# The last two sums of a 64x64 inverse: from identity products on TensorE and copies on ScalarE to additions on VectorE

## The chip, the core and the metric

The kernel runs on one core of one Trainium2 chip. The metric is the device time in microseconds (us) of one execution. A time is the median of the runs shown; the profile is of one execution more, with its own time and span. A core has five engines with a queue each, worked off in order: TensorE (PE in the rows; PEld is its loading of stationary operands), VectorE (DVE), ScalarE (ACT), GpSimd (POOL) and SyncE (SP), which issues the loads and stores.

## What is computed

Two trunk layers over 1024 latent and 256 context tokens. In each layer one input projection feeds a retention head group and an RWKV-7 head group; their gated outputs go through one output projection. The change lies in the RWKV-7 scan, which the reference writes as one step per token:

```
def step(s, inp):
    r_t, w_t, k_t, v_t, kap_t, a_t = inp
    s_kap = jnp.einsum('bhvk,bhk->bhv', s, kap_t)
    s = (s * w_t[:, :, None, :]
         - s_kap[..., None] * (kap_t * a_t)[:, :, None, :]
         + v_t[..., None] * k_t[:, :, None, :])
    return s, jnp.einsum('bhvk,bhk->bhv', s, r_t)
...
    s_fin, y = lax.scan(step, s0, xs, reverse=reverse)
```

## The kernel before

The scan is done in chunks of 64 tokens. Within a chunk the dependence of each token on the earlier ones is a triangular 64x64 system, whose inverse is worked out ahead of the scan. A head pair has 10 steps (of two chunks, two directions and two heads: eight inverses side by side, four matrices of 128 partitions by 64 columns); there are four head pairs and two layers, so 80 steps in all.

Three functions make a step. `prep` loads features and scales them. `prep2` multiplies them (`pm`, then `gq`), and inverts. `seq` is the recurrence proper: it multiplies with the state, takes `z2`, the finished inverse, and updates `uv` and the state `st`. `prep2` runs three steps ahead of `seq`, on two lanes in turn: a lane has one PSUM bank `pinv`, whose halves are `q` and `tp`. Between the steps the program deals out the projections (`pproj`, lines 493 to 495) and the other work of the layer as filling.

The inverse goes like this. The matrix (I plus `gq`) is split into two f16 parts `hi` and `lo`. Six levels build an approximate inverse in f16: line 1001 multiplies `hi` into `tz`, VectorE masks the bank to `xx` (line 1015), line 1017 multiplies with `ttb`, ScalarE copies to `tz` (line 1018), VectorE transposes to `tt` (lines 1021 and 1028). Then the remainder is formed: line 1030 makes the product of `hi` and `lo` with `tz`, less the identity, in the bank, and ScalarE writes its negative to `eb` (line 1033). Two corrections follow: `z1 = tt + e^T tt` and `z2 = tt + e^T z1`. Each of these two sums is done by the helper `one_sum`: a 128x256 product of the identity `one16` with `tt` opens the bank (line 990), four 128x64 products with `eb` add to it (line 993), and ScalarE copies the bank to `z1` (f16) or `z2` (f32). Rows of the profile name both of these tiles `z`, since they leave trailing numbers out; line 1037 is `z1` and line 1040 is `z2`.

The order of instructions on each engine is laid out when the program is built, by a scheduler that picks among ready work by a timeline of its own; `prep2` and `seq` are given priority over the filling.

Of the kernel before, what the change touches and what calls it, by code (L numbers as in the profile page):

```python
# [12 lines left out]
F16 = mybir.dt.float16  # L13
AF = mybir.ActivationFunctionType
ALU = mybir.AluOpType
# [110 lines left out]
def hybrid_kernel(ctx: ExitStack, tc: tile.TileContext, a: dict, out: bass.AP, dbg: dict | None = None):  # L126
    nc = tc.nc
# [3 lines left out]
    const = ctx.enter_context(tc.tile_pool(name="const", bufs=1))  # L131
# [7 lines left out]
    def bank(tag, name):  # L139
        return ps.tile([128, 512], F32, tag=tag, name=name, bufs=BANKS[tag])  # L140
# [6 lines left out]
    def behind(ins, first):  # L147
        tc.add_manual_dep(ins.ins, first.ins.name, mybir.DependencyInfo(mybir.DependencyClass.NoSync, mybir.DependencyReason.DATA),
                          reason="the first product of a bank clears its written bits")
# [15 lines left out]
    def x_tile(tb):  # L165
        t = ln_pool.tile([128, D], F32, tag="xt", name="xt", bufs=XTB)
        load(t, a["ctx"][0, 128 * tb:128 * tb + 128, :] if tb < 2 else a["x"][0, 128 * (tb - 2):128 * (tb - 2) + 128, :])
        return t
# [4 lines left out]
    def cload(name, shape):  # L173
        t = const.tile(shape, F32, name=name)
        load(t, a[name])
        return t

    ident = cload("c_id", [128, 128])
# [7 lines left out]
    kdix = cload("c_kd", [128, 4])  # L186
    keep = cload("c_rs", [128, 256])
    id16 = const.tile([128, 64], F16, name="id16")
    one16 = const.tile([128, 128], F16, name="one16")
    neg16 = const.tile([128, 128], F16, name="neg16")  # L190
    nc.vector.tensor_copy(one16, ident)
    nc.vector.tensor_scalar(neg16, ident, -1.0, None, ALU.mult)
    lvm = const.tile([128, 2, 6, 64], F16, name="lvm")
    nc.vector.tensor_copy(id16[0:64], ident[0:64, 0:64])
# [32 lines left out]
    def turn(key):  # L227
        at[key] += 1
        return ring[key][(at[key] - 1) % len(ring[key])]
# [144 lines left out]
    for l in range(DEPTH):  # L374
# [55 lines left out]
        if l == 0:  # L430
            lp = ln_pool
            stage = [lp.tile([128, 8, 128 * len(tiles)], F32, name=f"xs{ci}") for ci, tiles in enumerate(LN_TILES)]
            for ci, tiles in enumerate(LN_TILES):
# [5 lines left out]
                for i, tb in enumerate(tiles):  # L439
                    t = x_tiles[tb] if tb < XTB else x_tile(tb)  # L440
# [7 lines left out]
                for k in range(8):  # L448
                    p = bank(("inv", "m")[k % 2], "pxt")
# [500 lines left out]
        def prep2(sp, c):  # L950
# [7 lines left out]
            for h in range(2):  # L958
                pm[h] = quad(bank("m", f"pm{h}"))
                for i in range(2):  # L960
                    for d in range(2):
                        nc.tensor.matmul(pm[h][:, i, d, 0:q1], bk[HR[h], i, d, :], own[HR[h], i, d, 0:q1],  # L962
                                         start=True, stop=True)
# [16 lines left out]
            q, tp = [pc[:, 256 * k:256 * k + 256].rearrange("p (i d t) -> p i d t", i=2, d=2) for k in range(2)]  # L980
            ID = [(i, d) for i in range(2) for d in range(2)]
# [6 lines left out]
            def one_sum(lhs, rhs, parts):  # L988

                one = nc.tensor.matmul(pc[:, 0:256], lhs, rhs, start=True, stop=False, skip_group_check=True)  # L990
                for n, (w, x) in enumerate(parts):
                    for i, d in ID:
                        behind(nc.tensor.matmul(q[:, i, d, :], w[:, i, d, :], x[:, i, d, :], start=False,
                                                stop=n == len(parts) - 1, skip_group_check=True), one)
# [3 lines left out]
            for n in range(6):  # L998
# [14 lines left out]
                else:  # L1013
# [5 lines left out]
                    if n < 5:  # L1019
                        tt = sp.tile([128, 2, 2, 64], F16, tag=f"tt{lane}", name="tt", bufs=1)  # L1020
# [10 lines left out]
            e = turn("eb")  # L1031
            for h in range(2):
                nc.scalar.activation(idr(e[HR[h], :, :, 64 * h:64 * h + 64]), idr(q[HR[h]]), AF.Copy, scale=-1.0)
            flat = lambda t: t.rearrange("p i d t -> p (i d t)")
            one_sum(one16, flat(tt), [(e, tt)])
            z1 = sp.tile([128, 2, 2, 64], F16, tag="z1", name="z1", bufs=1)
            nc.scalar.copy(z1, q)
            one_sum(one16, flat(tt), [(e, z1)])
            z2 = sp.tile([128, 2, 2, 64], F32, tag="z2", name="z2", bufs=ZB)
            nc.scalar.copy(z2, q)  # L1040
            c.update(gq=gq, bt=bt, z2=z2)

        def seq(sp, cur, nxt, st, ys):
# [200 lines left out]
        def ahead(g):  # L1244
            p, s = divmod(g, NT)
            if p < NP:
                need(p, ready)
                stages[g] = prep(sp, p, s)
            if 0 <= g - 1 < NP * NT:
                with tc.high_priority(offset=1000):  # L1250
                    prep2(sp, stages[g - 1])
# [64 lines left out]
```

## Time and profile before

| | |
|---|---|
| median of 3 runs | 2461.8 us (2458.17 to 2465.19) |
| profiled execution | 2462.74 us, of which the span from first to last instruction is 2460.7 us |
| TensorE busy | 2299.2 us, 93% of the span |
| VectorE, ScalarE, GpSimd busy | 1735.6, 1414.8 and 1319.7 us (71%, 57%, 54%) |
| mean granted TensorE clock | 0.964 |

A busy time is the union of an engine's instructions. A matmul's row lasts from its start to the end of its results, so consecutive matmuls overlap in the rows; what a matmul holds back is the distance from its start to the next start. A wait is idle time of an engine and is put down to what ended last before it.

### The profile page before, as it was taken

The numbers are of one execution on the slowest core, as the hardware profiler recorded it, in microseconds if no ns is written. First come the engines' busy times: TensorE is split into PE (matmuls) and PEld (weight loads), VectorE is DVE, ScalarE is ACT, GpSimd is POOL, SyncE is SP. The second block draws the span as 40 slices with busy tenths as digits, with TensorE's granted clock in tenths as the row PEclk, the third lists the DMA queues.
The fourth block names the chain that finished last, engine by engine and source line by source line (L and its number), as shares of the span: only waits on it lengthen the run. The fifth ranks groups of instructions, "written<-read, shape, count | busy, mean of one in ns | idle before, by whom it ended". The sixth has DMA issues, their size and how long they took to land.

```text
span 2460.7 us, 69593 instructions
## 1 busy us (share of the span) xinstructions
PE 2299.2 (93%) x25463; PEld 1739.9 (71%) x25463; DVE 1735.6 (71%) x4784; ACT 1414.8 (57%) x4261; POOL 1319.7 (54%) x2032
## 2 busy tenths in 40 slices
PE   5779999999999999999997899999999999998997
PEld 2357776877788777778655687778768877776855
DVE  2646686787678867777648677767867886669756
ACT  3455664565566655456546666646655665456663
POOL 1455564465556654456536556545654665456662
PEclk7888999999999999999998899999999999999998
DMA  8754443334334423335533543434433443334544
GB/s 313 270 187 110 117 118 87 113 108 124 78 89 139 126 70 92 75 100 154 176 108 123 152 130 112 108 94 119 128 87 100 124 124 80 79 88 120 143 130 128
DMA packets 539606, 302.77 MB, mean 123 GB/s; under 512 B 238995, under 2 KB 526465, under 8 KB 537217
## 3 DMA queue, kind: packets, MB, share of 16 engines
q1 hardware_dynamic: 539264, 298.33, 42.1%
q8 instruction: 201, 3.29, 0.6%
q14 instruction: 141, 1.15, 0.2%
HBM read 212.21 MB, written 85.98 MB: 121 GB/s over the span
## 4 chain that ended last, share of the span: by engine, by line
PE 58%; DVE 13%; DMA 6%; ACT 4%; issue 3%; POOL 2%; SPq 2%; DVEq 0%; POOLq 0%; ACTq 0%
PE pproj L493 8%; PE pproj L495 8%; PE pproj L494 8%; PE pseq L1061 8%; PE pm L962 5%; DMA ft<-feat 2%; PE pseq L1053 2%; PE pinv L1001 2%; PE pinv L1017 2%; PE pout L821 1%; PE pout L823 1%; PE pss L638 1%; PE pout L822 1%; PE pss L648 1%; PE pyt L1127 1%
## 5 line engine op out<-in xcount | busy, mean ns | idle before, releaser
L493 PE MATMUL pproj<-h_hi,whi 128*128 128x256 f16 (+2 forms) x2128 | 631.3, 298 | 9.1 <-ACT craw L505 5.1
L494 PE MATMUL pproj<-h_lo,whi 128*128 128x256 f16 (+2 forms) x2128 | 629.1, 297 | 7.6 <-DVE h_lo L365 7.1
L495 PE MATMUL pproj<-h_hi,wlo 128*128 128x256 f16 (+2 forms) x2128 | 627.2, 297 | 0.7 <-POOL wlo L320 0.7
L320 POOL TENSOR_TENSOR wlo<-wraw,whi 128x256 f16<-128x256 f32 x360 | 250.5, 707 | 208.7 <-ACT wraw L319 181.0
L495 PEld LDWEIGHTS <-wlo 128*128 128x128 f16 x2128 | 213.5, 100 | 76.5 <-issue 12.1
L494 PEld LDWEIGHTS <-whi 128*128 128x128 f16 x2128 | 212.6, 100 | 77.6 <-issue 18.6
L493 PEld LDWEIGHTS <-whi 128*128 128x128 f16 x2128 | 213.1, 100 | 75.3 <-issue 10.4
L986 POOL COPY ttb<-tt 64x256 f16<-64x256 f16 x320 | 139.1, 436 | 205.2 <-DVE tt L1021 160.5
L1015 DVE TENSOR_TENSOR xx<-pinv,lvm 128x256 f16<-128x256 f32 x400 | 164.3, 416 | 90.6 <-PE pinv L1001 87.4
L318 ACT ACTIVATE whi<-wraw 128x256 f16<-128x256 f32 x360 | 139.2, 412 | 132.9 <-PE pproj L494 61.1
L1018 ACT CAST tz<-pinv 128x256 f16<-128x256 f32 x400 | 146.1, 370 | 119.9 <-PE pinv L1017 107.7
L962 PE MATMUL pm<-own,bk 64*128 64x128 f32 (+1 forms) x1280 | 201.6, 294 | 8.3 <-DVE bk L942 4.0
L1021 DVE STREAM_TRANSPOSE tt<-tz 128x256 f16<-128x256 f16 x320 | 139.4, 437 | 97.0 <-ACT tz L1018 94.3
L976 POOL TENSOR_TENSOR il<-gq,c_id 64x256 f32<-64x256 f32 x160 | 120.1, 751 | 133.1 <-DVE gq L965 119.3
L986 ACT COPY ttb<-tt 64x256 f16<-64x256 f16 x320 | 128.6, 402 | 106.5 <-DVE tt L1021 102.1
L962 PEld LDWEIGHTS pm<-own,bk 64*128 64x128 f32 x1280 | 163.2, 193 | 33.1 <-issue 8.6
L965 DVE TENSOR_TENSOR gq<-pm,c_m 128x256 f32<-128x256 f32 (+1 forms) x320 | 115.7, 402 | 50.6 <-PE pm L962 49.8
L1061 PE MATMUL pseq<-st,own 64*64 64x64 f32 x2432 | 149.4, 228 | 0.0
L319 ACT ACTIVATE wraw<-wraw 128x256 f32<-128x256 f32 x376 | 146.3, 410 | 3.9
L1001 PEld LDWEIGHTS <-hi 128*128 128x128 f16 x1920 | 104.6, 99 | 41.6 <-issue 9.7
L1012 POOL TENSOR_TENSOR lo<-il,hi 64x256 f16<-64x256 f32 x160 | 113.5, 710 | 36.8 <-ACT hi L977 28.0
L1008 POOL TENSOR_TENSOR ttb<-hi,lvm 128x256 f16<-128x256 f16 x160 | 113.6, 729 | 19.0 <-ACT hi L977 18.2
(255 smaller groups left out, 5906.7 us busy)
## 6 DMA issues: line engine op xcount, KB each, us to landing
ft<-feat SPq DMA_DIRECT2D x320, 160.0 KB
wraw<-in_w_in_dram SPq DMA_DIRECT2D x264, 128.0 KB
feat<-zth SPq DMA_DIRECT2D x80, 256.0 KB
wm<-in_w_mod_dram SPq DMA_DIRECT2D x16, 1024.0 KB
wraw<-in_w_out_dram SPq DMA_DIRECT2D x112, 128.0 KB
lap<-la SPq DMA_DIRECT2D x40, 256.0 KB
uv<-vt SPq DMA_DIRECT2D x320, 32.0 KB
wm<-in_w_mod_dram SPq DMA_DIRECT2D x16, 512.0 KB
```

What stands on the lines that cost most here:

```text
L319: nc.scalar.activation(raw, raw, AF.Copy, scale=WS)
L320: nc.gpsimd.tensor_tensor(lo, raw, hi, ALU.subtract)
L493: nc.tensor.matmul(p[:, 0:n], hi[:, k, :], h_hi[:, kk, m0:m1], start=first, stop=False)
L494: nc.tensor.matmul(p[:, 0:n], hi[:, k, :], h_lo[:, kk, m0:m1], start=False, stop=False)
L495: nc.tensor.matmul(p[:, 0:n], lo[:, k, :], h_hi[:, kk, m0:m1], start=False, stop=stop)
L962: nc.tensor.matmul(pm[h][:, i, d, 0:q1], bk[HR[h], i, d, :], own[HR[h], i, d, 0:q1], start=True, stop=True)
L986: eng(idr(dst[HR[h], :, :, 64 * h:64 * h + 64]), idr(src[HR[h]]))
L1001: nc.tensor.matmul(q[:, i, d, :], hi[:, i, d, :], id16 if n == 0 else tz[:, i, d, :], start=True, stop=True)
L1015: nc.vector.tensor_tensor(xx, q, mk, ALU.mult)
L1018: nc.scalar.copy(tzn, tp)
L1021: nc.vector.transpose(idr(tt), idr(tzn))
L1061: rm = nc.tensor.matmul(pq[HR[h], k, d, :], lhs, rhs, start=False, stop=stop, skip_group_check=True)
```

## The change

The identity product is left out of both sums. The four products with `eb` now open the bank themselves, and VectorE adds bank and `tt` into `z1` and `z2`, where ScalarE had copied the bank. `one16` and the copy that fills it go; the first sum, with `neg16`, stays as it is.

```
-    one16 = const.tile([128, 128], F16, name="one16")
     neg16 = const.tile([128, 128], F16, name="neg16")
-    nc.vector.tensor_copy(one16, ident)
...
-            flat = lambda t: t.rearrange("p i d t -> p (i d t)")
-            one_sum(one16, flat(tt), [(e, tt)])
+            for i, d in ID:
+                nc.tensor.matmul(q[:, i, d, :], e[:, i, d, :], tt[:, i, d, :], start=True, stop=True)
             z1 = sp.tile([128, 2, 2, 64], F16, tag="z1", name="z1", bufs=1)
-            nc.scalar.copy(z1, q)
-            one_sum(one16, flat(tt), [(e, z1)])
+            nc.vector.tensor_tensor(z1, q, tt, ALU.add)
+            for i, d in ID:
+                nc.tensor.matmul(q[:, i, d, :], e[:, i, d, :], z1[:, i, d, :], start=True, stop=True)
             z2 = sp.tile([128, 2, 2, 64], F32, tag="z2", name="z2", bufs=ZB)
-            nc.scalar.copy(z2, q)
+            nc.vector.tensor_tensor(z2, q, tt, ALU.add)
             c.update(gq=gq, bt=bt, z2=z2)
```

The scheduler lays out every queue anew, so places shift all over the program. Line numbers after the change are two lower up to the inverse's end, and one lower behind it.

On TensorE, at the first correction of the tenth inverse of the first layer, the queue before the change reads so (`whi` is a weight of the projections, `eb` the remainder):

```order
L494 LDWEIGHTS whi
L494 MATMUL pproj<-h_lo,whi 128x256
L990 LDWEIGHTS one_97
L990 MATMUL pinv<-tt,one_97 128x256
L993 LDWEIGHTS eb_1780
L993 MATMUL pinv<-tt,eb_1780 128x64
```

And at the same correction after it (`pyt` belongs to the readout of an earlier step):

```order
L493 LDWEIGHTS wlo
L493 MATMUL pproj<-h_hi,wlo 128x256
L1126 MATMUL pyt<-c_id,yc 64x64 x3
L1033 LDWEIGHTS eb_1778
L1033 MATMUL pinv<-tt,eb_1778 128x64
```

The weight load of `one` and its product are gone, and the four products with `eb` stand directly behind other work.

On VectorE, at the end of the same inverse, before the change, no instruction of the two sums stands in the queue (`uv` and `st` are the recurrence, `kkd` and `gs` the retention and gate work, `yc` and `yb` the readout):

```order
L1081 COPY uv<-pseq 64x2x64
L688 SCALAR_TENSOR_TENSOR gs<-gth,pproj 128x256
L1093 SCALAR_TENSOR_TENSOR st<-pseq,f,sf 128x64 x2
L1098 TENSOR_TENSOR ym<-pseq,ym 128x64 x2
L1113 TENSOR_TENSOR yc<-ym,gsm 128x128
L618 SCALAR_TENSOR_TENSOR sbp_1799<-sbp_1798,cd,sbp_1799 128x64
L1113 TENSOR_TENSOR yc<-ym,gsm 128x128
L1138 TENSOR_TENSOR yb<-yb,bo 128x256
```

After the change the two additions (`z_5787` is `z1`, `z_5793` is `z2`) stand among these:

```order
L1080 COPY uv<-pseq 64x2x64
L1112 TENSOR_TENSOR yc<-ym,gsm 128x128 x2
L1035 TENSOR_TENSOR z_5787<-pinv,tt 128x256
L686 SCALAR_TENSOR_TENSOR gs<-gth,pproj 128x256
L1137 TENSOR_TENSOR yb<-yb,bo 128x256
L1092 SCALAR_TENSOR_TENSOR st<-pseq,f,sf 128x64 x2
L1097 TENSOR_TENSOR ym<-pseq,ym 128x64 x2
L616 SCALAR_TENSOR_TENSOR sbp_1797<-sbp_1796,cd,sbp_1797 128x64
L1138 SCALAR_TENSOR_TENSOR yb<-yb,gt 128x256
L1039 TENSOR_TENSOR z_5793<-pinv,tt 128x256
L963 TENSOR_TENSOR gq<-pm_6154,c_m_88 128x256 x2
```

`z1` now stands ahead of the state's update `st`, and `z2` ahead of the masking `gq` of a later step.

## Rows read from the trace of the kernel before

**Rows 1.** The page: busy by engine, then 40 slices, then the chain.

```profile
PE 2299.2 (93%) x25463; PEld 1739.9 (71%) x25463; DVE 1735.6 (71%) x4784; ACT 1414.8 (57%) x4261; POOL 1319.7 (54%) x2032
...
PE   5779999999999999999997899999999999998997
...
PE 58%; DVE 13%; DMA 6%; ACT 4%; issue 3%; POOL 2%; SPq 2%; DVEq 0%; POOLq 0%; ACTq 0%
```

**Rows 2.** Busy time by stretch: the two layers' scan stretches, all engines.

```profile
182.00:1247.00 1065.00, 1033.86 (x12078) 808.19 (x12078) 779.92 (x2215) 624.00 (x1902) 592.38 (x920) 0.98 0.39 110
1387.00:2412.00 1025.00, 984.91 (x11321) 753.31 (x11323) 755.52 (x2111) 617.49 (x1887) 588.45 (x918) 0.98 0.40 111
```

**Rows 3.** Timeline of PE, 417.2 to 418.2 us: start, duration, engine, line.

```profile
417.25 0.27 PE L494 MATMUL pproj<-h_lo,whi 128*128 128x256 f16 x1
417.36 0.28 PE L1017 MATMUL pinv<-xx,ttb 128*128 128x64 f16 x4
417.48 0.27 PE L495 MATMUL pproj<-h_hi,wlo 128*128 128x256 f16 x1
417.59 0.27 PE L493 MATMUL pproj<-h_hi,whi 128*128 128x256 f16 x1
417.70 0.27 PE L990 MATMUL pinv<-tt,one 128*128 128x256 f16 x1
417.81 0.28 PE L993 MATMUL pinv<-z,eb 128*128 128x64 f16 x4
418.02 0.39 PE L1053 MATMUL pseq<-uv,gq 128*64 128x64 f32 x6
```

**Rows 4.** Line 990, the identity products: count, nanoseconds min/median/max.

```profile
L990 PEld LDWEIGHTS <-one x160: 94/98/180, 218.3 to 2411.2; 128*128 128x128 f16 x160
L990 PE MATMUL pinv<-tt,one x160: 269/273/437, 218.5 to 2411.5; 128*128 128x256 f16 x160
```

**Rows 5.** Tile pinv: the readers of the bank, nanoseconds min/median/max.

```profile
L1015 DVE TENSOR_TENSOR xx<-pinv,lvm x400: 377/417/427, 184.2 to 2398.5; 128x256 f16<-128x256 f32 x134
...
L1037 ACT CAST z<-pinv x80: 347/372/406, 219.3 to 2410.5; 128x256 f16<-128x256 f32 x80
L1040 ACT COPY z<-pinv x80: 348/372/418, 227.4 to 2411.9; 128x256 f32<-128x256 f32 x80
```

**Rows 6.** Waits of PE, 182 to 2412 us: total us, times, longest.

```profile
PE pinv L1017 <- DVE xx L1015: 7.9, 13, 1.4
PE pseq L1061 <- DVE uv L1081: 7.0, 8, 2.5
...
PE pinv L1001 <- ACT tz L1018: 5.6, 9, 1.0
...
PE pinv L990 <- ACT z L1037: 0.9, 3, 0.5
```

**Rows 7.** Tile pseq: the recurrence's copy to uv on DVE.

```profile
L1081 DVE COPY uv<-pseq x160: 292/293/294, 232.2 to 2425.1; 64x128 f32<-64x128 f32 x160
```

**Rows 8.** Waits of ACT, whole span: total us, times, longest.

```profile
ACT z L1040 <- PE pinv L993: 30.7, 31, 3.0
...
ACT z L1037 <- PE pinv L993: 17.3, 21, 2.9
```

**Rows 9.** Busy time by stretch: where VectorE is fullest, as in rows 2.

```profile
680.00:820.00 140.00, 140.00 (x1756) 116.38 (x1752) 115.80 (x342) 87.20 (x255) 81.71 (x119) 1.00 0.40 112
1840.00:2000.00 160.00, 154.86 (x1927) 129.50 (x1927) 130.83 (x380) 102.33 (x313) 94.85 (x144) 1.00 0.40 111
```

**Rows 10.** Busy time by stretch around one spell of low granted clock.

```profile
1030.00:1037.00 7.00, 5.51 (x93) 4.56 (x93) 6.83 (x26) 3.67 (x12) 3.79 (x7) 0.99 0.56 133
1037.00:1058.00 21.00, 20.70 (x160) 15.76 (x161) 11.40 (x31) 8.73 (x32) 7.50 (x13) 0.52 0.16 45
```

## The prediction

> **What bounds the kernel now.** I read the page first: TensorE is busy 93% of the span, its slices are full from the fourth to the end but for the turn between the layers, and the chain that ended last runs through it for 58% [rows 1]. The reader should not stop at that figure, because a matmul's row overlaps the next. So the second view is busy time by stretch. In the two scan stretches, 2090 us together, TensorE shows nothing running in 71.2 us (1065 - 1033.9 and 1025 - 984.9); VectorE is busy 1535 us there, 73.5%, ScalarE 1241 us, 59%; both have room on average [rows 2]. In a full stretch, 680 to 820 us, TensorE has no gap at all [rows 9]. The third view is the timeline, for what a product really holds back: 128x256 products start 0.11 us after each other though each row lasts 0.27, and they do so without pause [rows 3]. Where a queue starts its work back to back, what is taken out of it comes off the time. The fourth view is TensorE's list of waits: its largest entries on the recurrence and the inverse are 7.9, 7.0 and 5.6 us in all [rows 6]. So in the stretches that the change touches TensorE's own work is the bound, with a few short waits on VectorE and ScalarE between.
>
> **The change part by part.** *The identity products.* 160 of them go, two in each of 80 steps [rows 4]. One holds back the next start by 0.11 us: 417.70 to 417.81 [rows 3]. The same rows show that nothing reappears in its place: line 1017 is also a set of four 128x64 products right behind a projection, and it starts 0.11 us after it and lets the next start 0.12 us later; its loads are covered by the product ahead. The load of `one` was covered as well, so its 0.098 us [rows 4] is worth nothing. Sum: 160 x 0.11 = 17.6 us less on TensorE. If the row's full 0.273 us counted it would be 43.7; I don't take that, since the next product starts long before.
>
> *The copies on ScalarE.* 160 x 0.372 = 59.5 us less [rows 5]. ScalarE is not the bound, and TensorE waited for the copy to `z1` three times, 0.9 us [rows 6]. What stands behind these copies gets earlier, `tz` above all, for which TensorE waits 9 times in 400 [rows 6]. At that frequency it is 160 x 9/400 x 0.37 = 1.3 us; I take zero, and 1.3 as the bound.
>
> *The additions on VectorE.* There are 160, each reading 128x256 f32 from the bank and 128x256 f16 from a tile. The trace has this form already: line 1015, 377 to 427 ns, median 417 [rows 5]. `z2` writes f32 in place of f16; the two copies on ScalarE, f16 and f32 out, both take 372 [rows 5], so I price it the same. That is 160 x 0.417 = 66.7 us more work, 0.83 us a step. Per link of the chain it is 0.045 us slower than the copy; twice a step, 7.2 us over all, if the inverse were the path; it runs three steps ahead of its use, so I count that at nothing.
>
> What of the 66.7 us comes to the path? First, TensorE can wait for the new result itself. For line 1015 that cost 7.9 us in 400, 0.02 each [rows 6]; 160 x 0.02 = 3.2 us. Second, what is queued behind: in the new order `z1` stands ahead of `st` and `z2` ahead of `gq`, with `uv` in the neighbourhood. TensorE was held by `uv` 8 times [rows 6] in 160 [rows 7], 5%. If an addition of 0.42 us stands before such a moment in each case, 160 x 0.05 x 0.42 = 3.4 us. Bounds: nothing, if the additions fall into VectorE's idle quarter; all 66.7, if each holds TensorE for its whole length. The first is much nearer to what line 1015 shows, so I take 6.6 us.
>
> *The fill of `one16`* is one small copy in the start-up, where VectorE is not full; nothing. The first sum with `neg16` is untouched.
>
> The sum: 2462.7 (the profiled execution) - 17.6 + 6.6 = 2451.7. The profiled execution lies 0.9 over the median of the runs, so I expect a median of **2451 us**, 0.4% less.
>
> [...]
>
> **The rivals.** *The work saved falls into gaps (no change).* If the step is paced by the recurrence through `w`, `uv` and `st`, or by the two lanes of the inverse, TensorE's queue only waits 0.11 us longer at the next product of the chain. For it: 71.2 us of gaps in the scan [rows 2], four times what is saved, and short waits below the length of a row that the busy time doesn't show. Against it: 680 to 820 us without a gap [rows 9]. If three quarters of the 17.6 us are lost so and the 6.6 us are paid, the time is 2462.7 - 4.4 + 6.6 - 0.9 = 2464; if nothing is paid, 2457.
>
> *VectorE's queue holds up the recurrence (slower).* The place is the additions in front of `uv` and `st`. ScalarE stood idle 30.7 and 17.3 us ahead of the two copies, waiting for the products [rows 8]; now VectorE's queue stands there, and everything behind it, in stretches where it is already busy 115.8 of 140 us [rows 9]; five to six steps there add 4.7 us, 86%. It cancels the gain when an addition keeps TensorE for 17.6/160 = 0.11 us on average, 26% of its length, and makes the kernel slower by 0.3% from (17.6 + 7.4)/160 = 0.156 us, 37%. At half of its length the time is 2461.8 - 17.6 + 33.4 = 2478. Against it: line 1015, in the same queue, costs 0.02 us each.
>
> *A larger gain.* The granted clock falls to half in spells: 0.52 from 1037 to 1058 us, behind 7 us in which TensorE was busy 5.5, and in these 21 us some 10 are lost [rows 10]. The new order can lose or add such a spell. With the whole 17.6 us, ScalarE's 1.3 and one spell less: 2461.8 - 28.9 = 2433. A spell more puts the forecast at 2461, among the no-change cases.
>
> **How the numbers follow.** What a measurement can tell from no change is 0.3%, 7.4 us: 2454.4 and 2469.2 are the limits. The forecast, 2442 to 2454, gets 0.56; the larger gain 0.07; work lost in gaps or a spell more 0.24; VectorE's queue 0.13. So faster 0.63, same 0.24, slower 0.13. The range from 2437 to 2469 leaves out most of the slower case and the far end of the larger gain, some 2 in 10.
>
> **What the profile after would show.** Right: 160 matmuls fewer; in the scan TensorE's starts 0.11 us apart with projection and `eb` products adjoining; VectorE's two lines at 0.42 us, busy total near 1802 us; ScalarE near 1355; TensorE's waits for VectorE up by less than 10 us. Wrong: waits of TensorE for `uv`, `st`, `xx` or the products with `z` grown by 20 us or more (the slower rival), or its gaps in the scan grown by as much as its work fell, with no single waiter (the no-change rival). The forecast fails if an addition takes far over 0.42 us, or if spells of low clock differ by more than one between the two traces.

## The result: 0.4 to 0.7% slower, and the profile after

The changed kernel takes 2477.5 us (median of 6 runs, 2470.6 to 2487.5) against 2459.7 us for the kernel before (6 runs): ratio 1.0074, 95% interval 1.0048 to 1.0101. A later comparison of the same queues (g0 below), 12 runs against 29 on one chip, gave 1.0042 [1.0018, 1.0065]. The prediction was 2451 us and faster; both the sign and the range (up to 2469) failed.

The page of the changed kernel: the line of busy times and the line of the granted clock in 40 slices.

```profile
PE 2309.5 (93%) x25303; PEld 1739.8 (70%) x25303; DVE 1746.0 (70%) x4943; ACT 1370.0 (55%) x4101; POOL 1321.3 (53%) x2032
...
PEclk7888999999999999999998899999999999988997
```

The reader is to see the work moved as the change says: 160 matmuls fewer than in [rows 1], ScalarE 45 us less. Yet TensorE's busy time is 10 us more, not less. Busy time grows when the clock falls, since each product lasts longer (a row of 258 columns takes 0.27 us at a granted clock of 1.00 and 0.42 us at 0.50, in the timeline below). The view of the cores shows the mean granted clock of the changed kernel:

```profile
core 0: 2477.6 us, clock 0.953
```

Before, 2460.7 us ran at 0.964. If all that ran in a low stretch went at half speed, the clock took the span times (1 - clock): 2477.6 x 0.047 = 116.4 us after, 2460.7 x 0.036 = 88.6 us before, 28 us more. The span grew by 17 only, so by this measure the rest of the kernel got 11 us shorter, which is the sum of the prediction (17.6 - 6.6 = 11.0). That agreement is luck in part: the measure charges 2.5 us for each 0.001 of clock, and the runs of one kernel show 1.7 (ahead of the table below). By that price the clock took some 18 us and the rest got some 2 us shorter. Busy time by stretch, for the same stretches as [rows 2] and the second of [rows 9] (PE, PEld, DVE, ACT, POOL, then the granted clock):

```profile
182.00:1247.00 1065.00, 1031.50 (x12016) 800.84 (x12015) 788.10 (x2297) 599.38 (x1824) 591.97 (x919) 0.99 0.40 109
1387.00:2412.00 1025.00, 985.17 (x11140) 751.05 (x11138) 750.56 (x2166) 595.62 (x1802) 589.83 (x916) 0.96 0.40 110
...
1840.00:2000.00 160.00, 159.99 (x1873) 131.27 (x1870) 126.45 (x379) 96.64 (x294) 90.50 (x135) 0.94 0.40 111
```

The first layer's scan is as it was, a little better in clock. Most of the loss is in the second layer's, where the clock fell from 0.98 to 0.96, and TensorE got through 11140 products where before it got through 11321, 181 fewer; only some 80 of these had been taken out there. From 1840 to 2000 us before had 1.00.

Tile pinv of the changed kernel, the two new additions (ns min/median/max), and the waits of TensorE from 182 to 2412 us (total, times, longest), which answer to [rows 5] and [rows 6]:

```profile
L1035 DVE TENSOR_TENSOR z<-pinv,tt x80: 385/418/427, 220.9 to 2416.3; 128x256 f16<-128x256 f32 x80
L1039 DVE TENSOR_TENSOR z<-pinv,tt x80: 384/416/427, 226.3 to 2417.2; 128x256 f32<-128x256 f32 x80
```

```profile
PE pseq L1060 <- DVE uv L1080: 6.6, 7, 2.7
...
PE pinv L1015 <- DVE xx L1013: 4.4, 9, 0.9
...
PE pinv L1037 <- DVE z L1035: 1.7, 3, 1.0
...
PE pinv L999 <- DVE z L1039: 1.3, 4, 0.6
```

The additions take the 0.417 us of the prediction, TensorE waits 3.0 us for them in all (3.2 were predicted), and the waits for `uv` and `xx` did not grow. TensorE shows nothing running for 73.3 us in the two scan stretches, 71.2 before. No wait explains the 17 us.

What one fall of the clock looks like: busy time by stretch, 1887 to 1905 us of the changed kernel, and the timeline of PE around the fall (start, duration, line).

```profile
1887.00:1890.00 3.00, 3.00 (x50) 2.51 (x47) 2.29 (x7) 2.28 (x6) 0.00 (x0) 1.00 0.14 45
1890.00:1892.50 2.50, 2.50 (x32) 2.18 (x29) 2.16 (x7) 0.73 (x3) 1.09 (x2) 1.00 0.55 160
1892.50:1895.00 2.50, 2.50 (x19) 1.76 (x18) 1.35 (x4) 0.77 (x2) 1.18 (x2) 0.76 0.17 58
1895.00:1902.50 7.50, 7.50 (x50) 6.22 (x50) 3.28 (x12) 1.81 (x5) 4.62 (x9) 0.50 0.12 35
```

```profile
1889.78 0.45 PE L1060 MATMUL pseq<-w,z 64*64 64x64 f32 x8
1890.16 1.10 PE L960 MATMUL pm<-own,bk 64*128 64x64 f32 x8
1891.19 0.45 PE L1060 MATMUL pseq<-st,own 64*64 64x64 f32 x8
1891.57 0.71 PE L636 MATMUL pss<-qt,kt 64*128 64x128 f32 x4
1892.12 0.38 PE L639 MATMUL pss<-sbp,qt 64*128 64x128 f32 x2
1892.43 0.23 PE L999 MATMUL pinv<-tz,hi 128*128 128x64 f16 x2
...
1893.54 0.27 PE L493 MATMUL pproj<-h_hi,wlo 128*128 128x258 f16 x1
...
1893.94 0.42 PE L493 MATMUL pproj<-h_hi,wlo 128*128 128x258 f16 x1
```

TensorE shows no gap in these 15.5 us (a row runs to the end of its results, so a pause shorter than a row would not show), and still the granted clock drops to half, 0.50 from 1895 to 1902.5 us. From 1889.78 to 1893.54 us stand narrow products only, 128 columns or fewer and nearly all f32, of the recurrence and the attention; the first wide one behind them still takes 0.27 us, and from 1893.94 us on they take 0.42.

This fall is not the usual one. The trace has sixteen falls between 182 and 2412 us, and in the 4 us ahead of fourteen of them TensorE stood idle for 0.4 to 3.5 us, as at 2187 us behind a wait of 1.38 us for VectorE. In the kernel before it stood idle for 0.8 to 3.3 us in the 4 us ahead of all ten ([rows 10] is one of them). So 2 of the 26 falls in these two traces have no such gap ahead, this one and the one at 1928 us.

### The profile page after: what moved, and what is told of

It is laid out like the page before. It is cut to its first block, busy times and chain, and to the rows that moved or that the text cites. A ratio compares the mean times of both kernels' runs of the same rounds, so it can differ in the third digit from the quotient of the medians.

```text
span 2477.6 us, 69184 instructions
## 1 busy us (share of the span) xinstructions
PE 2309.5 (93%) x25303; PEld 1739.8 (70%) x25303; DVE 1746.0 (70%) x4943; ACT 1370.0 (55%) x4101; POOL 1321.3 (53%) x2032
## 5 line engine op out<-in xcount | busy, mean ns | idle before, releaser
L999 PE MATMUL pinv<-tz,hi 128*128 128x64 f16 x1600 | 112.7, 195 | 10.0 <-DVE tz L1002 6.0
```

The costliest lines, as they stand in the source:

```text
L999: nc.tensor.matmul(q[:, i, d, :], hi[:, i, d, :], id16 if n == 0 else tz[:, i, d, :], start=True, stop=True)
```

## The experiments

Two things could explain this: the scheduler laid every queue out anew (the prediction gave that no price), or the change itself costs, by VectorE or by the clock. To part them, most kernels below hold all instructions that two kernels share to the places that they have in one kernel's queues. The program is built once for its order, and then again with an edge between neighbours of each engine's queue:

```diff
+    _, queues = program(*DONOR, None)
+    nc, got = program(*TARGET, queues)
...
+                for q in queues.values():
+                    for x, y in zip(q, q[1:]):
+                        tc.add_manual_dep(told[y], told[x].name, _mybir.DependencyInfo(_mybir.DependencyClass.NoSync, _mybir.DependencyReason.DATA),
```

Only the identity products, the copies and the additions differ then. "Old order" has the queues of the kernel before, "new order" those of the changed kernel.

The results together. "Clock" is the mean over a kernel's runs. "At full clock" is the mean over runs of time times clock; it counts every low stretch as if all in it went at half speed, 2.5 us for each 0.001 of clock. That is too much: over the 254 runs, taken within each kernel, the time falls by 1.68 +- 0.07 us for each 0.001 ("+-" is one standard error throughout). So differences stand below at both prices, "at full clock" and "at equal clock", which is the difference of the mean times less 1.68 us for each 0.001 by which the clocks differ. As most falls stand behind a wait (24 of the 26 above), which costs time of its own, it is not shown that even the smaller price is the clock's alone.

The kernel before stood in each of the four comparisons at 2459 to 2461 us, clock 0.963 to 0.9645, at full clock 2370 to 2371. Each comparison had a chip of its own: f1, f2, f3 and g1; g0, g2 and g3; d1, k1 and DUE 31; e1, e3 and RAMP 6.

| kernel | order | identity products, sum by | median us | ratio to before [95%] | clock | at full clock |
|---|---|---|---|---|---|---|
| g0, the change | new | none, VectorE | 2473.3 | 1.0042 [1.0018, 1.0065] | 0.9553 | 2362.6 |
| g1 | new | one, ScalarE | 2472.7 | 1.0057 [1.0039, 1.0074] | 0.9608 | 2375.3 |
| g2 | new | one useless, VectorE | 2470.7 | 1.0036 [1.0018, 1.0054] | 0.9607 | 2372.7 |
| g3 | new | one useless, 32 columns, VectorE | 2466.7 | 1.0021 [1.0000, 1.0041] | 0.9568 | 2359.4 |
| f1, the change | old | none, VectorE | 2466.0 | 1.0033 [1.0014, 1.0052] | 0.9578 | 2362.5 |
| f2 | old | one useless, VectorE | 2465.1 | 1.0020 [1.0003, 1.0038] | 0.9622 | 2370.4 |
| f3 | old | none, ScalarE (tt not added) | 2455.5 | 0.9979 [0.9960, 0.9998] | 0.9597 | 2355.7 |
| d1 | old | two, ScalarE | 2457.9 | 1.0009 [0.9992, 1.0025] | 0.9666 | 2377.1 |
| k1 | old | none, GpSimd | 2502.0 | 1.0193 [1.0171, 1.0215] | 0.9502 | 2378.4 |
| e1 | its own | one useless, VectorE | 2484.6 | 1.0098 [1.0079, 1.0117] | 0.9566 | 2376.4 |
| e3 | its own | none, ScalarE (tt not added) | 2471.4 | 1.0042 [1.0024, 1.0060] | 0.9563 | 2362.9 |
| before, RAMP 6 | its own | one, ScalarE | 2477.3 | 1.0074 [1.0054, 1.0095] | 0.9578 | 2373.8 |
| after, RAMP 6 | its own | none, VectorE | 2471.3 | 1.0051 [1.0034, 1.0069] | 0.9543 | 2359.1 |
| before, DUE 31 | its own | one, ScalarE | 2467.9 | 1.0053 [1.0030, 1.0075] | 0.9596 | 2368.9 |
| after, DUE 31 | its own | none, VectorE | 2490.4 | 1.0132 [1.0106, 1.0158] | 0.9460 | 2354.1 |

**Parts of the change, order free.** e1 puts useless identity products back into the changed kernel; e3 takes its sums back to plain copies on ScalarE (the addition of tt is left out).

```diff
+            nc.tensor.matmul(pc[:, 0:256], one16, flat(tt), start=True, stop=True)
```

```diff
-            nc.vector.tensor_tensor(z1, q, tt, ALU.add)
+            nc.scalar.copy(z1, q)
...
-            nc.vector.tensor_tensor(z2, q, tt, ALU.add)
+            nc.scalar.copy(z2, q)
```

> The additions stay on VectorE, but the 160 identity products are issued as well, as work without use (the four products with eb then open the bank anew and overwrite them). Clock theory (the full-width products kept TensorE's granted clock up; without them it falls in more spells): mean granted clock back at 0.960 or more, time 2455 to 2468, under that of the change in spite of 17.6 us more work. VectorE theory (the additions hold up the recurrence): slower than the change by the work put back, about 2495. Order theory (the new order of the queues alone made the time): anything from 2445 to 2490, and clock and time bear no relation to the products.

> The identity products are gone, and the bank is copied by ScalarE as before; the addition of tt is left out, so z1 and z2 lack it. Clock theory: mean granted clock 0.950 to 0.958 and 2468 to 2485, like the change. VectorE theory: 2440 to 2448, the 17.6 us of TensorE's work come off in full. Order theory: anything from 2445 to 2490.

e1 came out at 1.0098 and e3 at 1.0042. e3 has only less to do than before and is still slower, so neither VectorE's load nor work on TensorE can be its reason. Both also have queues of their own, and so neither prices a part.

**A number of the planner.** RAMP 6 in place of 5, in both kernels; no operation changes.

```diff
-RAMP = 5.0
+RAMP = 6.0
```

> The kernel before with one number changed that touches no operation (RAMP 6.0 in place of 5.0, a little more filling behind each of the first four steps of a layer); the scheduler lays the queues out anew, with as many rows moved as by the change. Clock and VectorE theories: 2455 to 2466, clock 0.960 to 0.967. Order theory: moves by 0.4% or more, above 2469 or below 2450.

> The changed kernel with the same number changed (RAMP 6.0 in place of 5.0), and so with another order. Clock and VectorE theories: 2470 to 2485, as the change; clock theory alone: clock 0.950 to 0.958. Order theory: at least 0.4% away from the change, below 2467 or above 2488.

The kernel before got 1.0074, as much as the change. In its trace the first product of the recurrence starts 7.2 us later (212.3 us in place of 205.1), but in the next step it is ahead (first product with `bt` at 231.2 us in place of 234.3), so no part of the 18 us can be put down to the later start. The changed kernel stays where it was with RAMP 5 (1.0051 beside 1.0042 and 1.0074). So the pair's sign is turned.

**The change on fixed queues.**

> The changed kernel, with every instruction that both kernels share held by fixed edges to the place that it has in the queues of the kernel before; the scheduler places only the 160 additions. Order theory (the new order of the queues made the loss, the change itself is as I summed it): 2440 to 2456. VectorE theory (the additions hold up the recurrence): 2468 to 2485. Clock theory (the missing full-width products let the granted clock fall): 2465 to 2480 with a mean clock of 0.958 or less.

> On the same fixed queues of the kernel before: the identity products are issued (without use), and VectorE adds. Beside the change on the same order it has 17.6 us more of TensorE's work. Order theory: 2458 to 2470, the copies' move alone at my 6.6 us. VectorE theory: 2485 to 2500. Clock theory: 2455 to 2465, clock 0.960 or more.

> On the same fixed queues: no identity products, ScalarE copies as before, and the addition of tt is left out. Order theory and VectorE theory: 2440 to 2448, TensorE's 17.6 us come off. Clock theory: 2465 to 2480, clock 0.958 or less.

> The other way round: the kernel before (identity products, copies on ScalarE) with all shared instructions held to the places that they have in the queues of the changed kernel. Order theory: slower than the changed kernel by what the change is worth, 2480 to 2495. VectorE theory and clock theory: 2455 to 2466, since the old sums are back.

g1 says that the new queues cost 0.57%, 13 us, with the old sums in them: nearly all that the change showed. On fixed queues the change costs 7 us (f1 against before) or nothing that can be told (g0 against g1, each beside before on its own chip, -0.5 +- 2.6 us between means). Taking the products out alone (f3) gives 5 us; f3 leaves out `tt`, so its numbers differ as well. VectorE's additions cost 4 us with the products in place (f2 against before) and some 12 without (f1 against f3). Of the three theories f1 fits the clock's alone, and f2 the order's and, at its edge, the clock's; f3 and g1 lie between the ranges of all three, so none of them holds by itself.

Where the 12 us lie is seen in the waits of TensorE from 182 to 2412 us (total, times, longest), f1 first, then f3:

```profile
PE pseq L1083 <- DVE uv L1103: 8.6, 8, 2.9
PE pinv L1027 <- DVE xx L1025: 7.3, 11, 1.4
PE pinv L1053 <- DVE z L1057: 5.1, 4, 3.0
...
PE pseq L1083 <- DVE uv L1103: 6.0, 7, 2.0
PE pinv L1027 <- DVE xx L1025: 4.3, 9, 0.9
PE pinv L1053 <- ACT z L1055: 0.8, 2, 0.5
```

All waits of TensorE for `uv`, `xx` and the two sums come to 23.0 us in f1 and 11.4 in f3, to 18.1 in f2 and 16.5 in the kernel before. On the new order they are 14.5 us in g0 and 14.2 in g1: there the additions hold TensorE up no more than the copies did. That is one trace each.

In every pair that differs by the wide identity products alone the clock is lower without them: f1 below f2 by 0.0043 +- 0.0012, f3 below before by 0.0040 +- 0.0011. One run of f1 comes out where the prediction had it, by luck. Its profiled execution, by the view of the cores, happened to get the clock of before:

```profile
core 0: 2450.3 us, clock 0.964
```

That is 10.4 us under the 2460.7 of before at 0.964, against the predicted 11. But it is the fastest of its 12 runs (2452.1 us with what lies around the span), whose clocks reach down to 0.950 and whose times reach up to 2481, and the 15 runs of before at 0.964 have a mean of 2459.4, 7 us more. All runs together put the change on this order at 2.6 +- 1.1 us less at equal clock, 7.5 us less at full clock.

**More identity products, and the sum on GpSimd.** d1 issues each identity product twice in the kernel before; k1 lets ScalarE copy the bank and GpSimd add.

```diff
+                    mine(nc.tensor.matmul(pc[:, 0:256], one16, flat(tt), start=True, stop=True))
```

```diff
-            nc.scalar.copy(z1, q)
+                    mine(nc.scalar.copy(zc, q))
+                    mine(nc.gpsimd.tensor_tensor(z, zc, tt, ALU.add))
```

> The kernel before with its queues as they are, and each of the 160 identity products issued twice (the second repeats the first; the result is the same), so TensorE has 160 products of 256 columns more, 17.6 us at the 0.11 us of the prediction. It is the opposite dose to the copies without identity products, which took 17.6 us out, came to 0.9979 and lowered the mean clock by 0.004. If the wide products hold the granted clock up, the mean clock rises to 0.966 or more and the time grows by less than the work, 2463 to 2470 us. If the clock answers only to chance, it stays at 0.963 to 0.964 and the time grows by what reaches the path: the 11 us that the removal was worth at equal clock, up to the whole 17.6, 2470 to 2477 us. If the products fall into gaps, there is no change.

> The queues of the kernel before; no identity products, ScalarE copies the bank to a tile as before and GpSimd adds the tile tt to it, so VectorE gets nothing. TensorE has 17.6 us less, GpSimd 160 additions more in a chain of its own behind each copy, some 0.7 us each by GpSimd's other 128 x 256 additions, an estimate. If VectorE's queue is what took the gain from the sums on VectorE (2466), this comes out near the copies without an addition, 2454 to 2460 us. If an extra link of 0.7 us in each block's chain costs as much as the load on VectorE, or GpSimd's queue holds its other work up, 2465 us or more. The mean clock is expected at 0.958 to 0.960, as in the other kernels without the products.

d1's timeline of PE, with the doubled product, and its stretches for [rows 10]:

```profile
416.36 0.28 PE L1048 MATMUL pinv<-tt,one 128*128 128x256 f16 x1
416.48 0.27 PE L998 MATMUL pinv<-tt,one 128*128 128x256 f16 x1
416.59 0.28 PE L1003 MATMUL pinv<-tt,eb 128*128 128x64 f16 x4
```

```profile
1030.00:1037.00 7.00, 6.83 (x98) 5.74 (x94) 5.51 (x15) 4.77 (x14) 5.06 (x9) 1.00 0.11 35
1037.00:1058.00 21.00, 18.93 (x254) 14.45 (x249) 17.04 (x55) 13.89 (x48) 11.26 (x19) 1.00 0.34 88
```

Each product holds back the next by 0.11 to 0.12 us, 17.6 us in all, and 7.0 us of that show at full clock, 5.5 at equal clock. But the clock rose by 0.0021 +- 0.0010, the low spell at 1037 us is not in this trace, and the time is the same, below the 2463 to 2470 us that the expectation gave for a risen clock. Work that nothing needs was done at no cost that can be told. k1 shows a link that does cost. The lines of GpSimd's addition and, from 182 to 2440 us, TensorE's waits:

```profile
L1059 POOL TENSOR_TENSOR z<-zc,tt x160: 657/668/954, 225.6 to 2452.5; 128x256 f16<-128x256 f32 x80, 128x256 f32<-128x256 f32 x80
```

```profile
PE pinv L1053 <- POOL z L1059: 34.9, 28, 3.0
...
PE pseq L1087 <- POOL z L1059: 6.1, 4, 4.2
```

TensorE waits 41 us for it, 22.7 us at full clock come out over f3, and the clock is the lowest on this order, 0.950 where 0.958 to 0.960 was expected. My expectation of 2454 to 2460 us was wrong: a copy and an addition of 0.67 us in each link of the inverse are too much. GpSimd's queue has a part in it: only 55 of the 160 additions found GpSimd idle, waiting for their copy. The two causes that the expectation named, the longer link and GpSimd's queue, are not told apart.

**The other number.** DUE 31 in place of 30 in both kernels.

```diff
-DUE = (30, 37)
+DUE = (31, 37)
```

> The kernel before with one number of its planner changed (DUE 31 in place of 30), no operation added or removed; the scheduler lays all queues out anew. If laying the queues out anew is by itself worth what the change showed, this moves by several us either way, 2450 to 2475 us. If the order matters little, within 0.3%: 2452 to 2467 us.

> The changed kernel with the same number of the planner changed (DUE 31 in place of 30). If the order that the changed kernel got by chance is the larger part of its 1.0074, this pair's difference between changed and unchanged is another than 18 us, and may turn its sign: the fixed orders put the change itself at 5 to 8 us. If the change itself costs 18 us, this stands 18 us above its partner without the change.

Before moves by 0.53% with nothing changed in its work. The changed kernel is 20 +- 4 us above its partner, as a change that costs 18 us would have it, although it is 15 us shorter at full clock and 3 at equal clock: its clock is 0.946 against 0.960. The pair with RAMP 6 differs by 6 us the other way, so neither pair prices the change.

**Useless products in the changed kernel.** g0 is the changed kernel held to its own queues; g2 adds the wide useless products, g3 the same with 32 columns.

```diff
+                        mine(nc.tensor.matmul(pc[:, 0:256], one16, flat(tt), start=True, stop=True))
```

```diff
+                        mine(nc.tensor.matmul(pc[:, 0:32], one16, flat(tt)[:, 0:32], start=True, stop=True))
```

> The changed kernel itself, every shared instruction held to its place in the changed kernel's queues: the same program as after, for a comparison on one chip. 2474 to 2480 us, mean clock 0.953 to 0.957.

> The changed kernel on its own queues, with the 160 identity products of 256 columns issued again ahead of the products with eb; the products after them start their bank anew, so that the identity's result is thrown away and VectorE adds tt as in the change. TensorE gets 17.6 us more of work that nothing needs. If the wide products hold the granted clock up, the mean clock rises by 0.004 or more over the changed kernel (0.958 to 0.962) and the time is the same or lower, 2468 to 2477 us. If they only cost what they take, the clock stays and the time is 8 to 18 us more, 2485 us or above.

> As the run with useless identity products, but each is 32 columns wide in place of 256: the same 160 instructions and weight loads, an eighth of the columns. If it is the work in the product that holds the clock up, the clock stays near the changed kernel's 0.954 and the time near its 2477 us, a few us more for the instructions. If only the place in the queue or the instruction matters, it goes as the full width does.

g2's clock is 0.0054 +- 0.0010 above g0's, and in spite of 10 us more at full clock (5.6 at equal clock) its time is no more (3.5 +- 2.2 us less). The stretch in which the changed kernel fell to half clock (its mean from 1885 to 1905 us is 0.74), in g2:

```profile
1885.00:1905.00 20.00, 20.00 (x234) 16.81 (x234) 15.54 (x50) 11.00 (x30) 10.32 (x15) 1.00 0.17 53
```

g3's clock is not clearly above g0's (0.0016 +- 0.0012) and is 0.0038 +- 0.0010 below g2's, as the work in the product would have it. But its time is 7.5 +- 2.5 us below g0's and 3 us less at full clock, for 160 instructions more. That was not expected, and why stays open.

## Why the prediction was wrong, point by point

- **What a removed product is worth (17.6 us).** At full clock 14.3 us (f3), 7.9 (f1 against f2), 10.0 (g0 against g2) and 7.0 (d1, doubled); at equal clock 11.4, 4.3, 5.6 and 5.5. So the reading of the timeline held in kind, as work taken out of TensorE's queue did come off, but the term was too large: a fifth to three quarters of it does not show. That this part lay in gaps, as the no-change rival had it, is likely and not shown. TensorE's own work was the bound for a part of the time only.
- **What the additions cost (6.6 us).** Their length and TensorE's own wait for them (3.0 us) were right in the changed kernel. The size depends on the order: the waits for `uv`, `xx` and the sums grow by 0.3 us on the new order (g0 against g1) and by 11.6 on the old one without the products (f1 against f3), where the additions cost 6.8 us at full clock and 8.7 at equal clock; with the products in place (f2 against before) they cost 0.4 and 1.7. The rival that VectorE's queue holds up the recurrence fell for the changed kernel, whose waits for `uv` did not grow; on the old order a part of it came true. VectorE's busy total was given as 1802 us and is 1746 in the new order, 1776 in the old one (f1's page); ScalarE's was given as 1355 and is 1370.
- **ScalarE's relief and the fill of `one16`, nothing:** no run speaks against it.
- **The step that failed: the clock.** The prediction had it as "a spell more" of some 10 us, by chance, and put that at 2461 us; it took the products' removal and the clock for independent of each other. In the profiled executions the clock took some 18 us more (28 if all in the low stretches went at half speed). On the same queues the change itself lowers the granted clock, by 0.0058 on the old order and by 0.0050 on the new one (each kernel beside before on its own chip). With queues of their own, changed and unchanged differ the same way (RAMP 6 0.0035, DUE 31 0.0136, g0 against before 0.0078), but there the order differs too. At 1.68 us for each 0.001 the 0.0050 to 0.0058 are 8 to 10 us. What the change gains at equal clock is 2.6 +- 1.1 us on the old order and 9.0 +- 1.5 on the new one (7.5 and 13.0 at full clock, where the clock takes 12 to 14). So on either order the clock takes about all of the gain or more. d1 and g2 show the same from the other side, with work put in. How the wide products hold the clock up is not shown.
- **The second step that failed: the new order had no price.** The section on the change and the prediction speak of a new order of the queues, and the sum takes the old and the new as equal. g1 prices that at 13 us, 8 of them at equal clock (5 at full clock), the rest clock. Orders got by a number that changes no work moved before by 11 us (DUE) and 18 us (RAMP).
- **The sum as it came.** By means of runs: order +12.7 us (g1) and the change on that order -0.5 (-9.0 at equal clock and +8.4 by the clock), some 12 us over before. That is what g0 shows; the first comparison shows 18.

Shown is that the new order costs most of what the change showed, that the wide products raise the clock on the same queues, and that by either price of the clock the change shortens what is left, by 3 to 9 us at equal clock where 11 were predicted. That the lower clock is what took this gain is worked out from the times of one kernel's runs (0.8 to 2.2 us for each 0.001 by single kernels, 1.68 over all); no run holds the clock still. Not settled is which feature of an order sets its clock, how the wide products raise it, nor why g3 is the fastest of the new order. The only kernel clearly under before, f3, leaves out the sum; no version with the whole computation beat before.

## What to carry to other kernels

Before pricing a few microseconds of work on a scheduled kernel, find out what the schedule alone does: change a number that alters no work, and hold the shared instructions to one order for the comparison. Read the granted clock beside every time, and price it by how the times of one kernel's runs follow their clocks; span times clock counted too much here, 2.5 us for each 0.001 where the runs showed 1.68. Wide products that look like waste can be nearly free, as they were here (d1 at 1.0009 of before, g2 3.5 +- 2.2 us under g0): measure what taking them out does to the clock as well as to the queue.

## What the runs showed of the hardware that was not expected

- The granted clock can fall while TensorE shows no gap: 15.5 of 15.5 us busy around 1892 us of the changed kernel, with narrow f32 products ahead of the fall. That is rare, 2 falls of 26 in the traces of before and after; in the 4 us ahead of the others TensorE stood idle for 0.4 to 3.5 us. Ahead of the fall at 1037 us of the kernel before [rows 10] it waited 0.59 us for ScalarE and 0.76 us for VectorE.
- The same program on the same queues gets another clock from run to run: f1 0.950 to 0.964, and 2481 to 2452 us with it. Over all kernels that is 1.68 us for each 0.001, two thirds of what half speed in every low stretch would cost.
- VectorE's busy time depends on the order. With the same instructions it is 1535.5 us in the two scan stretches before [rows 2] and 1496.8 us in the same stretches of g1. Groups by line, of g1 (its line 948 is line 940 of before, where the same 80 took 49.7 us, 622 ns each):

```profile
L948 DVE TENSOR_TENSOR own<-ft,ep 128x256 f32<-128x256 f32 x80 | 43.4, 542 | 17.8 <-PE pseq L1083 11.4 <-ACT ep L938 5.7
```
